# Attention's values as the stationary operand, two key heads in one bank, and mLSTM sums a step later

## The chip, the cores and the metric

The kernel runs on one core of a Trainium2 chip. The metric is the device time of one execution in microseconds (us). Five engines work side by side: TensorE (PE in the profile; its weight loads are PEld), VectorE (DVE), ScalarE (ACT), GpSimd (POOL) and SyncE (SP), which issues nearly all DMAs. Each engine takes its instructions in the order in which they stand, and waits where an operand isn't there.

## What is computed

A decoder trunk of two layers on 256 tokens of width 1024, in float32. The change lies in the mixer of each layer, between the two feed-forward blocks:

```python
u = rmsnorm(x); z = u @ W_in                       # q, k, v, gates of both mixers, merge gates
hA = mlstm(...)                                    # 4 heads, 128 values each
yA = (sigmoid(o) * rmsnorm(hA)) @ w_a
# sliding-window attention, 8 query heads, 2 key heads, 64 wide, window 128
m = max(max(logits), sink); pr = exp(logits - m)
denom = sum(pr) + exp(sink - m)
hB = einsum('bnkgqs,bnskd->bnqkgd', pr / denom, v)
yB = hB @ w_b
x = x + (sigmoid(gA) * yA + sigmoid(gB) * yB) @ W_out
```

## The kernel before

**Tiles.** The 256 tokens are two tiles of 128 (t = 0, 1). Every large product runs as three TensorE passes in a rounded float32 format (`mm_unit`): each weight matrix is loaded in units of up to 128x2048 (`raw`), ScalarE rounds it to `hi`, VectorE takes the rest as `lo`, and lo·xh + hi·xl + hi·xh is summed in PSUM. The stationary operand is the activation, turned so that features lie on the partitions; the moving one is 512 weight columns. `take` keeps three units ahead (`AHEAD = 3`); three raw buffers and four hi/lo buffers go round.

**Order.** TensorE's instructions stand in the order in which the code issues them. After each half unit (12 matmuls of one token tile) `stream` calls `tick`, which moves every spawned generator on by one `yield`. So side work (attention, mLSTM) is strewn between the halves of the projections, and the constants `W_...` say how many such steps a piece waits. The other engines' instructions are placed by the framework's scheduler, and then run in that order.

**The mixer.** `mix_in` projects `sq`, `if` (gates, keys, values), `mqk`, `mv`, `mo`, `ga0`, `ga1`, `gb0`, `gb1` (two units each, whose results are `z_mix_...`), then `w_b` (`yb`) and `w_a` (`ya`) for each half of the columns, then `w_out`. Beside the projections:

- Attention: `swa` normalises q and k, `swa_logits` multiplies them (`lg`, `L`), `swa_part` does the softmax. Token tile 0 is one part (8 heads, 128 keys), tile 1 two parts of four heads (256 keys, two key blocks kt). The probabilities `L` are turned to have keys on partitions: VectorE transposes 32x32 blocks into `inq_PT`, a DMA writes them to DRAM (`scr_PT`), a second reads them back in another order (`back_PT`), and a copy on ScalarE or VectorE puts them into `PT`. Of `back` there are two buffers, so that a second reading waits for the copy of the one before the last. Then `PT` is stationary and 64 columns of the values `vsw` move (`ov`, L721), one matmul for each head and key block. `hb` = `ov` times 1/denominator, and `hb` goes through the same turn (`inq_hb`, `scr_hb`, `back_hb`) before it is split into `abT`, the stationary operand of `yb`.
- mLSTM: `ml_mix` makes the weights `E` (E01, E2) from `st`; `ml_out` multiplies them by the values (`num`), divides, normalises (sums of squares `ssn`, with a GpSimd power `rn`), gates (`ha`), and turns `ha` through DRAM into the other half of `abT`, for `ya`.

`drain` finishes whatever is left of the generators ahead of `yb`.

Of the kernel before, what the change touches and what calls it, by code (L numbers as in the profile page):

```python
# [28 lines left out]
SWKV = 2  # L29
# [27 lines left out]
W_PT = 3  # L57
W_OV = 2
W_HB = 1
W_ST = 2  # L60
W_NUM = 1
W_HA = 3


@with_exitstack
def trunk_kernel(ctx: ExitStack, tc: tile.TileContext, a: dict, out: bass.AP):
# [50 lines left out]
    def by_cols(w, rows, cols, name):  # L117
# [48 lines left out]
    for i in range(DEPTH):  # L166
# [3 lines left out]
        for n in range(2):  # L170
            cols = [(512 * n, 512 * (n + 1))]
            specs.extend(by_cols(a["w_b"][i], 512, cols, f"wb{i}_{n}"))
            specs.extend(by_cols(a["w_a"][i], 512, cols, f"wa{i}_{n}"))
# [6 lines left out]
    def load_next(between=()):  # L180
# [8 lines left out]
        if between:  # L189
            src = srcs[0].rearrange("(k p) c -> p k c", p=P)  # L190
            for h, also in enumerate(between):
                ks = slice(h * kk // len(between), (h + 1) * kk // len(between))
                nc.sync.dma_start(rv[:, ks, :], src[:, ks, :])
                also()
        else:
            c0 = 0
            for s in srcs:
                w = s.shape[1]
                nc.sync.dma_start(rv[:, :, c0 : c0 + w], s.rearrange("(k p) c -> p k c", p=P))
                c0 += w  # L200
# [316 lines left out]
    def mix_in(pool, i, xn, finish):  # L517
# [127 lines left out]
        def swa_logits(t):  # L645
# [27 lines left out]
            for h0, L, mx in parts:  # L673
                gen = swa_part(t, h0, nh, L, mx)
                spawn(gen)
                advance(gen)

        def swa_part(t, h0, nh, L, mx):
            part = slice(h0, h0 + nh)
# [18 lines left out]
            rinv = stat("rinv")  # L698
            nc.vector.reciprocal(rinv, rs)
            for _ in range(W_PT):  # L700
                yield
# [11 lines left out]
            for _ in zip(*[turn_p(kt, j0) for kt in range(t + 1) for j0 in range(0, nh, 4)], strict=True):  # L713
                yield
            for _ in range(W_OV):
                yield
            ov = bank(f"ov{nmp}")[:, 0 : nh * HD]
            for j in range(nh):
                g = (h0 + j) // 4
                for kt in range(t + 1):  # L720
                    nc.tensor.matmul(  # L721
                        ov[:, j * HD : (j + 1) * HD],
                        PT[:, kt, j, :],
                        vsw[kt][:, g * HD : (g + 1) * HD],
                        start=kt == 0,
                        stop=kt == t,
                    )
            hb = work.tile([P, nh * HD], F32, tag="sg", name=f"hb{nmp}")
            nc.vector.tensor_tensor(
                heads(hb, HD), heads(ov, HD), rinv[:, :, None].broadcast_to([P, nh, HD]), op=ALU.mult  # L730
            )
            for _ in range(W_HB):
                yield
            ks = slice(h0 * HD // P, (h0 + nh) * HD // P)
            hi, lo = (part[:, ks, :] for part in abT[t][1])
            yield from back_split(blocks(hb), hi, lo, f"hb{nmp}")

# [87 lines left out]
        def ml_out(t, ha, E01, E2):  # L825
# [36 lines left out]
            nc.vector.tensor_tensor(haf, haf, go, op=ALU.mult)  # L862
# [189 lines left out]
```

## Time and profile before

| | |
|---|---|
| median of 3 runs | 1116.51 us (1115.41 to 1116.57) |
| profiled execution | 1116.3 us, of it 1114.4 us from first to last instruction |
| PE busy | 1101.9 us, 99% |
| DVE busy | 760.0 us, 68% |
| ACT busy | 585.7 us, 53% |
| DMA | 253.40 MB, 227 GB/s |
| mean granted TensorE clock | 0.998 |

The mixer of the first layer runs from about 200 to 350 us, that of the second from about 750 to 900. A row of the timeline gives the start in us from the span's start, the length of the group, engine, line, operation, tiles and shape; what stands in square brackets is idle time of that engine just before, with what ended it. Matmuls overlap in their records, so the time a matmul costs is the distance to the next one's start.

### The profile page before, as it was taken

The page shows a single profiled execution, that of the slowest core. Times are in us where ns is not written, and L with a number is a line of the kernel's source. Part 1 is how long each engine was busy: PE and PEld are TensorE (multiplying, and loading weights), DVE is VectorE, ACT ScalarE, POOL GpSimd, SP SyncE. Part 2 cuts the span into 40 slices and gives each one's busy share as a digit, 9 for nine tenths or more (in the row PEclk, how much of TensorE's full clock was granted, in tenths as well). Part 3 has the DMA queues.
Part 4 walks back from the last instruction along what each step waited for, and adds up shares of the span by engine and source line. Part 5 has one row for each costly group of instructions (what it writes and reads, how often), then busy time and mean ns, then how long its engine had stood idle before and what let it go on. Part 6 is the DMA issues. An engine that isn't in the chain of part 4 may idle for free.

```text
span 1114.4 us, 13451 instructions
## 1 busy us (share of the span) xinstructions
PE 1101.9 (99%) x5080; PEld 911.4 (82%) x5080; DVE 760.0 (68%) x962; ACT 585.7 (53%) x848; POOL 32.0 (3%) x30
## 2 busy tenths in 40 slices
PE   8999999999999999999999999999999999999998
PEld 7788888878878888888888888888787888888887
DVE  6775755689777666656776667556986777667564
ACT  6544544668545544444664454446784454445353
POOL 1000000100000000000000000001000000000000
PEclk9999999999999999999999999999999999999999
DMA  7888766777664867766757767666777557777661
GB/s 269 275 293 254 231 215 198 235 246 258 223 211 153 280 220 259 234 209 230 256 164 240 260 219 236 219 208 208 257 247 247 191 187 243 250 231 242 209 218 66
DMA packets 173026, 253.40 MB, mean 227 GB/s; under 512 B 18601, under 2 KB 72993, under 8 KB 172961
## 3 DMA queue, kind: packets, MB, share of 16 engines
q1 hardware_dynamic: 172960, 252.54, 68.9%
q8 instruction: 40, 0.66, 0.2%
q14 instruction: 26, 0.21, 0.1%
HBM read 228.64 MB, written 23.88 MB: 227 GB/s over the span
## 4 chain that ended last, share of the span: by engine, by line
PE 80%; DVE 10%; DMA 4%; issue 2%; ACT 2%; POOL 1%; SPq 0%; DVEq 0%
PE h_f L231 14%; PE h_f L233 14%; PE h_f L232 14%; PE acc_f_o L233 7%; PE acc_f_o L232 7%; PE acc_f_o L231 7%; DMA back_PT<-scr_PT 2%; PE acc_wout L233 1%; PE acc_wout L231 1%; PE acc_wout L232 1%; PE acc_pg L232 1%; PE acc_pg L233 1%; PE acc_pg L231 1%; DVE lo_z_ga L204 1%; DVE inq_PT L264 1%
## 5 line engine op out<-in xcount | busy, mean ns | idle before, releaser
L204 DVE TENSOR_TENSOR lo_f<-raw_f,hi_f 128x1024 fp32r<-128x1024 f32 (+1 forms) x176 | 207.6, 1215 | 83.6 <-ACT hi_f L203 83.1
L203 ACT CAST hi_f<-raw_f 128x1024 fp32r<-128x1024 f32 (+1 forms) x178 | 176.4, 1038 | 142.4 <-PE h_f L233 94.1
L204 DVE TENSOR_TENSOR lo_f_o<-raw_f_o,hi_f_o 128x1024 fp32r<-128x1024 f32 x88 | 104.2, 1219 | 71.1 <-ACT hi_f_o L203 71.1
L231 PE MATMUL h_f<-lo_f,xT_f_0h 128*128 128x512 f32 x352 | 138.0, 392 | 0.3 <-DVE lo_f L204 0.2
L232 PE MATMUL h_f<-hi_f,xT_f_0l 128*128 128x512 f32 x352 | 137.1, 390 | 1.1 <-DVE xT_f_0l L248 1.1
L231 PE MATMUL h_f<-lo_f,xT_f_1h 128*128 128x512 f32 x352 | 137.2, 390 | 0.5 <-DVE lo_f L204 0.4
L233 PE MATMUL h_f<-hi_f,xT_f_0h 128*128 128x512 f32 x352 | 137.0, 389 | 0.0
L232 PE MATMUL h_f<-hi_f,xT_f_1l 128*128 128x512 f32 x352 | 136.9, 389 | 0.0
L233 PE MATMUL h_f<-hi_f,xT_f_1h 128*128 128x512 f32 x352 | 136.9, 389 | 0.0
L203 ACT CAST hi_f_o<-raw_f_o 128x1024 fp32r<-128x1024 f32 x88 | 88.0, 1048 | 89.5 <-PE acc_f_o L233 52.9
L231 PEld LDWEIGHTS h_f<-lo_f,xT_f_0h 128*128 128x128 f32 x352 | 66.1, 188 | 15.0 <-issue 0.6
L231 PEld LDWEIGHTS h_f<-lo_f,xT_f_1h 128*128 128x128 f32 x352 | 66.1, 188 | 14.9 <-DVE lo_f L204 1.4
L232 PEld LDWEIGHTS h_f<-hi_f,xT_f_0l 128*128 128x128 f32 x352 | 66.1, 188 | 14.8 <-DVE xT_f_0l L248 1.4
L233 PEld LDWEIGHTS h_f<-hi_f,xT_f_1h 128*128 128x128 f32 x352 | 66.1, 188 | 13.8
L233 PEld LDWEIGHTS h_f<-hi_f,xT_f_0h 128*128 128x128 f32 x352 | 66.1, 188 | 13.7
L232 PEld LDWEIGHTS h_f<-hi_f,xT_f_1l 128*128 128x128 f32 x352 | 66.1, 188 | 13.7
L233 PE MATMUL acc_f_o<-hi_f_o,hT_f_1h 128*128 128x512 f32 x176 | 68.5, 389 | 0.0
L231 PE MATMUL acc_f_o<-lo_f_o,hT_f_0h 128*128 128x512 f32 x176 | 68.5, 389 | 0.0
L232 PE MATMUL acc_f_o<-hi_f_o,hT_f_0l 128*128 128x512 f32 x176 | 68.5, 389 | 0.0
L233 PE MATMUL acc_f_o<-hi_f_o,hT_f_0h 128*128 128x512 f32 x176 | 68.5, 389 | 0.0
L231 PE MATMUL acc_f_o<-lo_f_o,hT_f_1h 128*128 128x512 f32 x176 | 68.5, 389 | 0.0
L232 PE MATMUL acc_f_o<-hi_f_o,hT_f_1l 128*128 128x512 f32 x176 | 68.5, 389 | 0.0
(352 smaller groups left out, 2036.1 us busy)
## 6 DMA issues: line engine op xcount, KB each, us to landing
raw_f<-in_ffn_wi_dram SPq DMA_DIRECT2D x79, 1024.0 KB, 5.4
raw_f_o<-in_ffn_wo_dram SPq DMA_DIRECT2D x40, 1024.0 KB, 5.2
scr_h_f<-inq_h_f SPq DMA_DIRECT2D x40, 256.0 KB, 4.0
back_h_f<-scr_h_f SPq DMA_DIRECT2D x40, 256.0 KB, 5.0
raw_f<-in_ffn_wi_dram SPq DMA_DIRECT2D x18, 512.0 KB, 4.2
raw_z_ga<-in_w_in_dram SPq DMA_DIRECT2D x8, 1024.0 KB, 5.5
raw_z_gb<-in_w_in_dram SPq DMA_DIRECT2D x8, 1024.0 KB, 7.4
raw_wout<-in_w_out_dram SPq DMA_DIRECT2D x8, 1024.0 KB, 4.9
```

What stands on the lines that cost most here:

```text
L203: nc.scalar.copy(hi[:, o:e], raw[:, o:e])
L204: (nc.gpsimd if between and o // step % 2 == 0 else nc.vector).tensor_tensor(lo[:, o:e], raw[:, o:e], hi[:, o:e].bitcast(F32), op=ALU.subtract
L231: nc.tensor.matmul(o, xh, wl[:, k, sl], start=start, stop=False)
L232: nc.tensor.matmul(o, xl, wh[:, k, sl], start=False, stop=False)
L233: nc.tensor.matmul(o, xh, wh[:, k, sl], start=False, stop=stop)
L264: nc.vector.transpose(inq[:, 0:n].rearrange(f"p (b {order}) -> p b k s", b=4, k=k), src.rearrange("p k (c b) -> p b k c", b=4),)
```

## The change

Four things change in each layer's mixer.

1. The division by the softmax denominator moves ahead of the turn: `L` is multiplied by `rinv` on VectorE (128x1024 elements, three times a layer).
2. `ov` is turned round: 64 value columns of one key head are stationary, and the four heads' probabilities (512 columns of `PT`) move. Key head 0 writes PSUM partitions 0 to 63, key head 1 partitions 64 to 127 of one bank, so that the result has features on partitions already. `hb`, its turn and its DMAs go; `split_evac` splits `ov` into `abT` straight from PSUM. Both parts of tile 1 are now needed for its one `ov` group.
3. Since features are now grouped by key head, the rows of `w_b` are loaded in that order: two DMAs of 64 partitions (512 KB each) for a unit, in place of one of 128.
4. Steps: `W_OV` 2 to 4, `W_NUM` 1 to 2, and the waits `W_HB` (1) and `W_HA` (3) go.

```diff
-W_OV = 2
-W_HB = 1
+W_OV = 4
 W_ST = 2
-W_NUM = 1
-W_HA = 3
+W_NUM = 2
...
+    def by_heads(w, cols, name):
+
+        c0, c1 = cols
+        return [(f"{name}_0", 0, 4, [w[256 * g : 256 * (g + 1), c0:c1] for g in range(SWKV)], c1 - c0)]
...
-            specs.extend(by_cols(a["w_b"][i], 512, cols, f"wb{i}_{n}"))
+            specs.extend(by_heads(a["w_b"][i], cols[0], f"wb{i}_{n}"))
...
+                if s.shape[0] < kk * P:
+                    rows = slice(HD * g, HD * (g + 1))
+                    nc.sync.dma_start(rv[rows, :, :], s.rearrange("(k p) c -> p k c", p=HD))
+                    continue
...
             nc.vector.reciprocal(rinv, rs)
+            nc.vector.tensor_tensor(L, L, rinv[:, :, None].broadcast_to([P, nh, L.shape[2]]), op=ALU.mult)
...
+            turned += [PT[:, :, j0 : j0 + 4, :] for j0 in range(0, nh, 4)]
+            if len(turned) < SWKV:
+                return
             for _ in range(W_OV):
                 yield
-            ov = bank(f"ov{nmp}")[:, 0 : nh * HD]
-            for j in range(nh):
-                g = (h0 + j) // 4
-                for kt in range(t + 1):
+            ov = bank(f"ov{i}_{t}")
+            for kt in range(t + 1):
+                for g in range(SWKV):
+                    rows = slice(g * HD, (g + 1) * HD)
                     nc.tensor.matmul(
-                        ov[:, j * HD : (j + 1) * HD],
-                        PT[:, kt, j, :],
-                        vsw[kt][:, g * HD : (g + 1) * HD],
-                        start=kt == 0,
-                        stop=kt == t,
+                        heads(ov, P)[rows], vsw[kt][:, rows], turned[g][:, kt], start=kt == 0, stop=kt == t
                     )
-            hb = work.tile([P, nh * HD], F32, tag="sg", name=f"hb{nmp}")
-            nc.vector.tensor_tensor(
-                heads(hb, HD), heads(ov, HD), rinv[:, :, None].broadcast_to([P, nh, HD]), op=ALU.mult
-            )
...
-            yield from back_split(blocks(hb), hi, lo, f"hb{nmp}")
+            split_evac(*abT[t][1], blocks(ov))
...
-            for _ in range(W_HA):
-                yield
             yield from back_split(blocks(haf), *abT[t][0], f"ha{i}_{t}")
```

How this moves instructions is shown at three places of the first layer; the second layer is the same.

**TensorE, around `ov`.** Before, tile 0's eight `ov` matmuls stand ahead of the projection `gb0`'s first half unit, and tile 1's sixteen one half unit further on:

```order
L233 MATMUL z_mix_ga_1_2256<-hi_z_ga_4_2117,xT_mix_1_1h 128x512
L721 MATMUL ov_0_0_2399<-vsw_0_1555,PT_0_0_2136 128x64 x8
L231 MATMUL z_mix_gb_0_2412<-lo_z_gb_0_2191,xT_mix_0_0h 128x512
L232 MATMUL z_mix_gb_0_2412<-hi_z_gb_0_2190,xT_mix_0_0l 128x512
L233 MATMUL z_mix_gb_0_2412<-hi_z_gb_0_2190,xT_mix_0_0h 128x512
```

With the change tile 0's two matmuls stand two half units later, and tile 1's four another half unit on, between the two halves of `gb0`'s second unit:

```order
L240 MATMUL z_mix_gb_0_2412<-hi_z_gb_4_2261,xT_mix_0_1h 128x512
L735 MATMUL ov_1_2475<-PT_1_0_2178,vsw_0_1555 64x512
L735 MATMUL ov_1_2475<-PT_1_4_2185,vsw_0_1555 64x512
L735 MATMUL ov_1_2475<-PT_1_0_2178,vsw_1_1556 64x512
L735 MATMUL ov_1_2475<-PT_1_4_2185,vsw_1_1556 64x512
L238 MATMUL z_mix_gb_1_2413<-lo_z_gb_4_2262,xT_mix_1_1h 128x512
```

The `num` groups stand one half unit later than before (12 matmuls): tile 0's behind the first half of `ga1`'s second unit, tile 1's behind its second half.

**VectorE, where the probabilities are turned and copied back.** Before, the transposes of tile 1 (`inq_PT_1_...`) stand close together, ahead of the products of the mLSTM weights (`E` with `st`):

```order
L795 TENSOR_TENSOR E_0_2144<-Mb_1568,maskb 128x512
L699 RECIPROCAL rinv_1_0_2079<-rs_1_0_2073 128x4
L264 STREAM_TRANSPOSE inq_PT_1_0_0_0_2176<-L_1_0_2042 128x512
L697 TENSOR_TENSOR rs_1_4_2088<-rs_1_4_2088,es_1_4_2085 128x4
L699 RECIPROCAL rinv_1_4_2094<-rs_1_4_2088 128x4
L264 STREAM_TRANSPOSE inq_PT_1_0_1_0_2179<-L_1_0_2042 128x512
L204 TENSOR_TENSOR lo_z_ga_4_2118<-raw_z_ga_4_2116,hi_z_ga_4_2117 128x1024 x2
L264 STREAM_TRANSPOSE inq_PT_1_4_0_0_2183<-L_1_4_2044 128x512
L264 STREAM_TRANSPOSE inq_PT_1_4_1_0_2186<-L_1_4_2044 128x512
L811 TENSOR_TENSOR E_0_2143<-E_0_2143,st_0_2217 128x2x128
```

With the change the last two transposes come behind the multiplies by `rinv` (three of them are above this piece), behind these products and behind the `lo` of another unit:

```order
L271 STREAM_TRANSPOSE inq_PT_1_0_1_0_2182<-L_1_0_2043 128x512
L813 TENSOR_TENSOR E_0_2146<-E_0_2146,st_0_2220 128x2x128
L813 TENSOR_TENSOR E_0_2146<-E_0_2146,st_1_2221 128x2x128
L813 TENSOR_TENSOR E_0_2146<-E_0_2146,st_0_2220 128x2x128
L211 TENSOR_TENSOR lo_z_gb_0_2194<-raw_z_gb_0_2192,hi_z_gb_0_2193 128x1024 x2
L813 TENSOR_TENSOR E_0_2146<-E_0_2146,st_1_2221 128x2x128
L821 TENSOR_TENSOR E_0_2147<-E_0_2147,st_0_2230 128x128
L821 TENSOR_TENSOR E_0_2147<-E_0_2147,st_1_2231 128x128
L821 TENSOR_TENSOR E_0_2147<-E_0_2147,st_0_2230 128x128
L271 STREAM_TRANSPOSE inq_PT_1_4_0_0_2186<-L_1_4_2045 128x512
L821 TENSOR_TENSOR E_0_2147<-E_0_2147,st_1_2231 128x128
L271 STREAM_TRANSPOSE inq_PT_1_4_1_0_2189<-L_1_4_2045 128x512
```

The last copy into `PT` (`PT_1_4`), without which tile 1's `ov` can't end, stood behind `num`'s divisions before, and ahead of mLSTM's normalisation. With the change it stands behind the whole normalisation of mLSTM's tile 0 and a `lo`:

```order
L847 RECIPROCAL r_0_2323<-dd_0_2322 128x2 x2
L848 TENSOR_TENSOR ha_0_2240<-num_0_0_2326,r_0_2323 128x256
L848 TENSOR_TENSOR ha_0_2240<-num_0_1_2335,r_0_2323 128x256
L854 TENSOR_SCALAR vn_0_2344<-ssn_0_2324 128x4
L858 SCALAR_TENSOR_TENSOR ha_0_2240<-ha_0_2240,rn_0_2346,mlg_1551 128x128 x4
L864 TENSOR_TENSOR ha_0_2240<-ha_0_2240,gates_0_1559 128x512
L211 TENSOR_TENSOR lo_z_gb_4_2416<-raw_z_gb_4_2414,hi_z_gb_4_2415 128x1024
L720 COPY PT_1_4_2185<-back_PT_1_4_1_0_2190 128x512
```

**SP, ahead of `yb`.** Before, six DMAs of `hb` (`scr_hb`, `back_hb`) stand between the weight loads of `w_b`, `w_a` and `w_out`:

```order
L199 DMA raw_wa_0_0_2533<-in_w_a_dram 128x4x512
L270 DMA scr_hb_0_0_2474<-inq_hb_0_0_2434 128x512
L274 DMA back_hb_0_0_2435<-scr_hb_0_0_2474 128x4x128
L199 DMA raw_wb_1_0_2572<-in_w_b_dram 128x4x512
L270 DMA scr_ha_0_2482<-inq_ha_0_2459 128x512
L270 DMA scr_hb_1_0_2507<-inq_hb_1_0_2476 128x256
L199 DMA raw_wa_1_0_2614<-in_w_a_dram 128x4x512
L270 DMA scr_hb_1_4_2509<-inq_hb_1_4_2479 128x256
L270 DMA scr_ha_1_2511<-inq_ha_1_2484 128x512
L274 DMA back_ha_0_2460<-scr_ha_0_2482 128x4x128
```

With the change they are gone, and the two halves of a `w_b` unit stand apart, the second behind the readings of tile 1's probabilities:

```order
L281 DMA back_PT_1_0_1_0_2183<-scr_PT_1_0_1_0_2214 128x4x128
L204 DMA raw_wb_0_0_2454<-in_w_b_dram 64x4x512
L281 DMA back_PT_1_4_0_0_2187<-scr_PT_1_4_0_0_2216 128x4x128
L281 DMA back_PT_1_4_1_0_2190<-scr_PT_1_4_1_0_2218 128x4x128
L204 DMA raw_wb_0_0_2454<-in_w_b_dram 64x4x512
L206 DMA raw_wa_0_0_2503<-in_w_a_dram 128x4x512
L277 DMA scr_ha_0_2369<-inq_ha_0_2354 128x512
L204 DMA raw_wb_1_0_2537<-in_w_b_dram 64x4x512
L281 DMA back_ha_0_2355<-scr_ha_0_2369 128x4x128
L204 DMA raw_wb_1_0_2537<-in_w_b_dram 64x4x512
```

More of the change, by code (lines that the diff above doesn't have):

```diff
@@ L196, in load_next @@
             c0 = 0
-            for s in srcs:
+            for g, s in enumerate(srcs):
                 w = s.shape[1]
+                if s.shape[0] < kk * P:
+                    rows = slice(HD * g, HD * (g + 1))
+                    nc.sync.dma_start(rv[rows, :, :], s.rearrange("(k p) c -> p k c", p=HD))
+                    continue
                 nc.sync.dma_start(rv[:, :, c0 : c0 + w], s.rearrange("(k p) c -> p k c", p=P))
@@ L653, in swa_logits @@
             parts = []
+            turned = []
             for h0 in range(0, SWQ, nh):
@@ L673, in swa_logits, with swa_part @@
             for h0, L, mx in parts:
-                gen = swa_part(t, h0, nh, L, mx)
+                gen = swa_part(t, h0, nh, L, mx, turned)
                 spawn(gen)
                 advance(gen)
-        def swa_part(t, h0, nh, L, mx):
+        def swa_part(t, h0, nh, L, mx, turned):
             part = slice(h0, h0 + nh)
@@ L714, in swa_part @@
                 yield
+            turned += [PT[:, :, j0 : j0 + 4, :] for j0 in range(0, nh, 4)]
+            if len(turned) < SWKV:
+                return
             for _ in range(W_OV):
                 yield
-            ov = bank(f"ov{nmp}")[:, 0 : nh * HD]
-            for j in range(nh):
-                g = (h0 + j) // 4
-                for kt in range(t + 1):
+            ov = bank(f"ov{i}_{t}")
+            for kt in range(t + 1):
+                for g in range(SWKV):
+                    rows = slice(g * HD, (g + 1) * HD)
                     nc.tensor.matmul(
-                        ov[:, j * HD : (j + 1) * HD],
-                        PT[:, kt, j, :],
-                        vsw[kt][:, g * HD : (g + 1) * HD],
-                        start=kt == 0,
-                        stop=kt == t,
-                    )
-            hb = work.tile([P, nh * HD], F32, tag="sg", name=f"hb{nmp}")
-            nc.vector.tensor_tensor(
-                heads(hb, HD), heads(ov, HD), rinv[:, :, None].broadcast_to([P, nh, HD]), op=ALU.mult
-            )
-            for _ in range(W_HB):
-                yield
-            ks = slice(h0 * HD // P, (h0 + nh) * HD // P)
-            hi, lo = (part[:, ks, :] for part in abT[t][1])
-            yield from back_split(blocks(hb), hi, lo, f"hb{nmp}")
+                        heads(ov, P)[rows], vsw[kt][:, rows], turned[g][:, kt], start=kt == 0, stop=kt == t
+                    )
+            split_evac(*abT[t][1], blocks(ov))
         cem = small.tile([P, 16], F32, tag="cem", name=f"cem{i}")
@@ L862, in ml_out @@
             nc.vector.tensor_tensor(haf, haf, go, op=ALU.mult)
-            for _ in range(W_HA):
-                yield
             yield from back_split(blocks(haf), *abT[t][0], f"ha{i}_{t}")
```

## The prediction

> **What bounds the kernel now.** I read the page's busy times first, then what PE waited for, then the mixer's timeline.
>
> ```profile
> PE 1101.9 (99%) x5080; PEld 911.4 (82%) x5080; DVE 760.0 (68%) x962; ACT 585.7 (53%) x848; POOL 32.0 (3%) x30
> ```
>
> PE is busy from end to end; time goes only where PE's own work shrinks or a wait of PE goes. The list of PE's waits (engine, line, who is waited for: us in total, times, longest) is headed by two that this change can touch:
>
> ```profile
> PE yb L231 <- ACT abT_1h L247: 2.1, 3, 1.1
> PE yb L232 <- DVE abT_1l L248: 1.9, 2, 1.0
> ```
>
> The first stage behind the mixers, `yb`, waits for the attention output `abT_1`. What that costs in all is seen from starts in PE's timeline, the first layer and then the second:
>
> ```profile
> 302.35 0.39 PE L231 MATMUL yb<-lo_wb,abT_1h 128*128 128x512 f32 x1
> 302.57 0.39 PE L232 MATMUL yb<-hi_wb,abT_1l 128*128 128x512 f32 x1
> ...
> 306.99 0.50 PE L232 MATMUL yb<-hi_wb,abT_1l 128*128 128x512 f32 x1 [0.97 <-DVE abT_1l L248]
> ...
> 309.48 0.50 PE L231 MATMUL yb<-lo_wb,abT_1h 128*128 128x512 f32 x1 [1.06 <-ACT abT_1h L247]
> ...
> 311.21 0.39 PE L231 MATMUL ya<-lo_wa,abT_0h 128*128 128x512 f32 x1
> ...
> 313.93 0.39 PE L231 MATMUL ya<-lo_wa,abT_0h 128*128 128x512 f32 x1
> 314.61 0.50 PE L232 MATMUL ya<-hi_wa,abT_0l 128*128 128x512 f32 x1 [0.29 <-DVE abT_0l L248]
> ```
>
> ```profile
> 851.49 0.39 PE L231 MATMUL yb<-lo_wb,abT_1h 128*128 128x512 f32 x1
> ...
> 856.62 0.80 PE L232 MATMUL yb<-hi_wb,abT_1l 128*128 128x512 f32 x1 [0.97 <-DVE abT_1l L248]
> ...
> 860.79 0.39 PE L231 MATMUL ya<-lo_wa,abT_0h 128*128 128x512 f32 x1
> ```
>
> A matmul of 512 columns costs 0.227 us (302.35 to 302.57). The 24 of `yb` should take 5.4 us. They take 8.9 in the first layer (302.35 to 311.21), 3.4 too many, and 9.3 in the second (851.49 to 860.79), 3.9 too many. Idle time proper is less than that. In the second layer the view by stages shows the rest (length, PE busy, its rows, granted clock, DMA):
>
> ```profile
> 851.90:856.60 4.70, 2.98 (x12) 1.00 0.51 184
> 856.60:860.10 3.50, 3.48 (x8) 0.52 0.70 249
> ```
>
> For 3.5 us after the waits the granted clock is 0.52, and only eight matmuls are done. At half speed 3.5 us do the work of 1.8, so a wait of PE can cost itself and 1.7 us more. The Trainium skill, "TensorE: Matmul & The Clock Gate" (section "What's actually happening"), puts this to a window of about 3.4 us with too little activity, which runs freely; the length agrees, and the first layer, with more idle time and no slow stretch, agrees with the chance in it.
>
> **The change, part by part.** *`ov` on PE.*
>
> ```profile
> 275.16 1.89 PE L721 MATMUL ov<-vsw,PT 128*128 128x64 f32 x16
> 276.86 0.48 PE L231 MATMUL z_mix_gb<-lo_z_gb,xT_mix_0h 128*128 128x512 f32 x1
> 277.18 0.39 PE L232 MATMUL z_mix_gb<-hi_z_gb,xT_mix_0l 128*128 128x512 f32 x1
> ...
> 279.70 3.68 PE L721 MATMUL ov<-vsw,PT 128*128 128x64 f32 x32
> 283.19 0.48 PE L231 MATMUL z_mix_gb<-lo_z_gb,xT_mix_0h 128*128 128x512 f32 x1
> ```
>
> Before: 1.70 + 3.49, and 0.09 behind each (276.86 to 277.18 in place of 0.227): 5.4 us a layer. Each plain-f32 matmul shows as two passes (8 matmuls, 16 rows). The trace has no column groups. Nearest are mLSTM's `st` products, which use 64 rows each, side by side:
>
> ```profile
> 256.85 0.39 PE L233 MATMUL z_mix_ga<-hi_z_ga,xT_mix_1h 128*128 128x512 f32 x1
> 257.17 0.49 PE L807 MATMUL st<-qkT 64*128 64x256 f32 x2
> ...
> 257.17 1.13 PE L807 MATMUL st<-qkT 64*128 64x256 f32 x8
> 258.14 0.61 PE L815 MATMUL st<-qkT 64*128 64x128 f32 x8
> 258.68 0.50 PE L231 MATMUL z_mix_ga<-lo_z_ga,xT_mix_1h 128*128 128x512 f32 x1
> 259.02 0.39 PE L232 MATMUL z_mix_ga<-hi_z_ga,xT_mix_1l 128*128 128x512 f32 x1
> ```
>
> Two start within 0.01 us, so they run together; eight of 256 columns, four pairs, take 0.97, of which about 0.1 is the start: 0.21 a pair and pass, so 0.43 for 512 columns. Going in and out costs 0.09 (256.85 to 257.17), 0.1 at the start, 0.1 at the end and 0.11 (258.68 to 259.02): 0.4 a visit. With pairs: tile 0 two passes, 0.85 + 0.4; tile 1 four, 1.7 + 0.4. That is 3.4 a layer, a gain of 2.0; **4.0 for both**. Bounds: nothing for the visit, 5.7; no pairing, -1.3 (below). I take the pairs, since row groups are the nearest thing and run so.
>
> *`hb` and its way through DRAM go.* Off PE, `abT` now needs only a ScalarE and a VectorE pass over `ov`, which ends near 287 us, 14 us ahead of `yb`. The `hb` DMAs no longer hold the `back` buffers and ScalarE's queue ahead of `hi_wb`. So the `yb` excess goes, 3.4 + 3.9, and with `ha` turned three steps sooner (W_HA) less the one of W_NUM, `ya`'s 0.68 for 0.23 and as much as 0.1 behind it: **7.9**. Next late would be `lo_wb`: the second half of its unit now waits on SP behind the last `back_PT` (about 281 us), and lands some 5 us later; with 2.4 us of VectorE it is there by 293, 8 us early. The extra DMA issues cost SP 0.4 each, under that cover. Bounds: 6 (one wait of some 2 us comes back) to 7.9.
>
> *Multiplies and later transposes.* The VectorE sum hardly changes: three multiplies are added; `hb`'s product, transposes and smaller splits go. The order matters. VectorE's timeline:
>
> ```profile
> 262.17 2.09 DVE L264 STREAM_TRANSPOSE inq_PT<-L 128x512 f32<-128x512 f32 x2
> 264.17 1.38 DVE L811 TENSOR_TENSOR E<-E,st 128x256 f32<-128x256 f32 x4
> ...
> 265.86 2.36 DVE L204 TENSOR_TENSOR lo_z_gb<-raw_z_gb,hi_z_gb 128x1024 fp32r<-128x1024 f32 x2
> ...
> 268.52 0.43 DVE L711 COPY PT<-back_PT 128x512 f32<-128x512 f32 x1
> ...
> 275.95 0.75 DVE L846 TENSOR_TENSOR ha<-num,r 128x256 f32<-128x256 f32 x2
> ...
> 281.00 0.43 DVE L711 COPY PT<-back_PT 128x512 f32<-128x512 f32 x1 [2.20 <-DMA back_PT<-scr_PT]
> ...
> 282.62 1.14 DVE L856 SCALAR_TENSOR_TENSOR ha<-ha,rn,mlg 128x128 f32<-128x128 f32 x4 [1.12 <-POOL rn L302]
> 283.80 0.69 DVE L862 TENSOR_TENSOR ha<-ha,gates 128x512 f32<-128x512 f32 x1
> ```
>
> Two of ScalarE's squares for the normalisation, one head each, and the way of a `back_PT` reading from issue to landing:
>
> ```profile
> 280.48 0.31 ACT L850 ACTIVATE jn<-ha 128x128 f32<-128x128 f32 x1
> ...
> 280.92 0.31 ACT L850 ACTIVATE jn<-ha 128x128 f32<-128x128 f32 x1
> ```
>
> ```profile
> DMA to landing us min/median/max: 2.6/5.0/5.8
> ```
>
> The last two transposes started at 262.17. Now three multiplies stand ahead of them (no such row; nearest is a `lo` of the same size, two in 2.36, so 3.4 for three, some tenths in doubt), the `E` products (264.17 to 265.86, 1.7) and a `lo` pair (2.3): they start at 269.6 and end near 272. Another `lo` pair follows, to 274.3, then the copy of tile 0's probabilities, done at 274.8 (it started at 268.52 before). It frees the `back` buffer that the second reading of tile 1's first part needs; that lands 2.6 to 5.8 us later, 277.4 to 280.6, and is copied in 0.43. Then, new in VectorE's order, comes the normalisation of mLSTM's tile 0: divisions 1.0, four squares on ScalarE 0.44 apart, 1.8, a small operation 0.2, GpSimd's power 1.1, `ha` 1.1, the gate 0.7, one `lo` 1.1, 7.0 in all. Then the last copy, done between 285.3 and 288.5.
>
> When does PE need it? Before, half a unit beside `ov` takes 2.8 (276.86 to 279.70); two halves behind 283.19 end at 288.75. Less 5.2 of the old `ov`, plus 1.25 of tile 0's new one, is 284.8, and tile 1's fourth matmul, which needs the copy, issues 0.2 + 0.85 later, near 285.9. So PE waits **0 to 2.6 us**, in both layers alike; less than nothing is excluded, since no wait of PE stands at `ov` now. The reading at 274.8 has only the tail of a 1 MB load ahead of it, which speaks for the lower half of its way: I take 1.0 a layer, **2.0 for both**. Behind the waiting matmul stand the rest of `gb0` and `gb1`, so the wait is paid in full.
>
> *`num`, a step later.* It started 1.4 us behind the end of the `E` products (264.17 + 1.38):
>
> ```profile
> 266.97 1.05 PE L838 MATMUL num<-vaug,E 128*128 128x129 f32 x8
> ```
>
> It now comes half a unit, 2.7, later; the products come 3.6 later (3.4 of multiplies and a `lo` pair of 2.3 ahead of the last, less two transposes of 2.1 now behind). That leaves 0.5: no wait, and 0.5 of one at the worst. The step itself only moves work that PE does anyway.
>
> **Sum**: 4.0 + 7.9 - 2.0 = 9.9 off the profiled execution's 1116.3 (1.9 of it outside the span), 0.2 below the median: **1106.4 us**. Own range 1103.0 (no wait at `ov`, visits nearly free) to 1109.6 (2.6 us of wait in each layer).
>
> **Rivals.** *Column groups don't pair.* Then each visit has twice the passes: 1.7 + 0.4 and 3.4 + 0.4, 5.9 for 5.4 before: a loss of 0.5 a layer, 5.0 worse than forecast: **1111.4**. For it: no such pair is in the trace. Against: `st`.
>
> *Bare loads.* If besides no weight load of a column group ran under a matmul, 12 loads a layer would come on top, each like this row's 188 ns:
>
> ```profile
> L231 PEld LDWEIGHTS h_f<-lo_f,xT_f_0h 128*128 128x128 f32 x352 | 66.1, 188 | 15.0 <-issue 0.6
> ```
>
> That is 4.5 more: **1115.9**. Against: 82% of PEld beside 99% of PE, which shows loads running under matmuls of the same rows all the time. The Trainium skill, "TensorE: Matmul & The Clock Gate" (Part 3, "The mechanism"), has the rule that gives this rival: a load overlaps matmuls in flight only where its row group differs, and column groups share theirs. The same part reports 2.38 times the speed for three column tiles, against both rivals; no run so far shows either.
>
> *The last copy is late by the whole bound*, 2.6, and the idle time brings the slow clock, 1.7: 4.3 a layer for 1.0, 6.6 worse: **1113.0**. For it: the second layer's slow stretch followed on waits of this size. Against: the median way of a reading, 5.0, includes readings behind large loads.
>
> *Slower.* The same mechanism further on: mLSTM's squares wait in ScalarE's order behind copies of `back_PT`, so that both readings and the 7 us run strictly behind one another. What is gained before it is 11.9, 5.9 a layer; with the slow clock it decides from a wait of 4.2 us. At 6 us (the copy at 292) each layer pays 7.7: **1119.8**. For it: all three are in one in-order queue; against: the readings would have to exceed their maximum of 5.8.
>
> *It doesn't free `yb`*: `lo_wb` or `ha` lands late and about 2 us a layer stay: **1110.4**.
>
> **How the numbers follow.** Forecast 0.63, no pairs 0.12, bare loads 0.03, late copy 0.12, slower 0.05, `yb` not freed 0.05. Range 1103.0 to 1112.5: from no wait at all and free visits (1104.4 less 1.6) past the unpaired case; it leaves out bare loads, the late copy and the slower case, 0.2. A measurement here tells about 0.2%, 2.2 us, from no change: below 1114.1 is faster. Forecast, no pairs, not freed and 0.08 of the late copy are faster, 0.88; the rest of the late copy and bare loads are within, 0.07; slower 0.05.
>
> **What would show it.** Right: `ov` rows in twos starting together, about 0.9 us for tile 0 and 1.7 for tile 1; no `yb` wait on `abT_1`; no stretch with a granted clock near 0.5 at 855; a wait of `ov` on DVE `PT` of about 1 us. Wrong: rows 0.43 apart one by one; `ov` waits above 2 us or a slow clock behind them; `yb` waiting for `lo_wb`.

## The result, and the profile after

The changed kernel takes **1109.38 us**, median of 4 runs (1108.48 to 1111.12); beside it on the same chip the kernel before takes 1116.54 (1115.41 to 1118.61, 4 runs). The ratio is **0.994, 95% interval 0.9924 to 0.9955**: 7.2 us faster, where 10.1 less than the median of before was forecast. It lies in the forecast's range, 3.0 us above the forecast itself. The profiled run is one of the four, the longest: 1111.12, with a span of 1109.3.

The page's first line of numbers, engines with busy time, share and instructions:

```profile
PE 1097.1 (99%) x5008; PEld 902.4 (81%) x5008; DVE 759.5 (68%) x954; ACT 585.6 (53%) x846; POOL 31.7 (3%) x30
```

PE still bounds the kernel and does 4.8 us less. The list of PE's waits (who is waited for: us in total, times, longest), from its top:

```profile
PE h_f L239 <- DVE xT_f_0l L255: 2.2, 1, 2.2
PE ov L735 <- DVE PT L720: 1.6, 2, 1.1
```

`yb` is gone from it, and `ov` has come in, waiting for the last copy of the probabilities, as forecast. The other row is in the first stage of the program. PE's timeline from the end of the mixer, first layer:

```profile
304.96 0.39 PE L238 MATMUL yb<-lo_wb,abT_1h 128*128 128x512 f32 x1
...
310.40 0.39 PE L238 MATMUL ya<-lo_wa,abT_0h 128*128 128x512 f32 x1
```

`yb` takes 5.44 us, 24 times 0.227, and no more. PE's timeline around `ov`, tile 0, then tile 1 in both layers:

```profile
283.49 0.39 PE L240 MATMUL z_mix_gb<-hi_z_gb,xT_mix_0h 128*128 128x512 f32 x1
283.81 1.08 PE L735 MATMUL ov<-PT,vsw 128*64 128x512 f32 x4
284.82 0.50 PE L238 MATMUL z_mix_gb<-lo_z_gb,xT_mix_1h 128*128 128x512 f32 x1
285.16 0.39 PE L239 MATMUL z_mix_gb<-hi_z_gb,xT_mix_1l 128*128 128x512 f32 x1
...
287.77 1.93 PE L735 MATMUL ov<-PT,vsw 128*64 128x512 f32 x6
290.20 1.07 PE L735 MATMUL ov<-PT,vsw 128*64 128x512 f32 x2 [0.50 <-DVE PT L720]
291.20 0.50 PE L238 MATMUL z_mix_gb<-lo_z_gb,xT_mix_1h 128*128 128x512 f32 x1
```

```profile
832.37 1.93 PE L735 MATMUL ov<-PT,vsw 128*64 128x512 f32 x6
835.36 1.07 PE L735 MATMUL ov<-PT,vsw 128*64 128x512 f32 x2 [1.06 <-DVE PT L720]
836.36 0.50 PE L238 MATMUL z_mix_gb<-lo_z_gb,xT_mix_1h 128*128 128x512 f32 x1
```

Tile 0's four passes are over in 1.01 us: two pairs. Tile 1's eight fall into six and two, with a wait between them.

Since the run as a whole moves by some us from one execution to the next, the stages are the better measure. They run here from the first matmul of one name to the first of another in PE's timeline (`gp` is the gates' transposes, ahead of everything that the change moves); "again" is a second profile of the changed kernel, from the experiments:

| stage, us | before | after | after, again |
|---|---|---|---|
| start to `gp`, layer 0 | 216.50 | 219.63 | 216.64 |
| `gp` to `yb`, layer 0 | 85.85 | 85.33 | 86.05 |
| `yb` to `ya` | 8.86 | 5.44 | 5.44 |
| `ya` to `tp_mx` | 11.49 | 10.88 | 10.88 |
| to `gp` of layer 1 | 442.96 | 442.92 | 442.89 |
| `gp` to `yb`, layer 1 | 85.83 | 85.89 | 86.16 |
| `yb` to `ya` | 9.30 | 5.44 | 5.44 |
| `ya` to `tp_mx` | 11.18 | 10.88 | 10.88 |
| to the end | 242.44 | 242.91 | 242.91 |
| span | 1114.4 | 1109.3 | 1107.3 |

The gain is all in `yb` and `ya`: 7.3 and 0.9. From `gp` to `yb`, where `ov` is cheaper and waits, the sum is nothing: -0.5 in the first profile, +0.5 in the second. And the first profile's start is 3.1 us later than before's.

### The profile page after: what moved, and what is told of

The parts are those of the page before. It is cut to its first block, busy times and chain, and to the rows that moved or that the text cites. A ratio compares the mean times of both kernels' runs of the same rounds, so it can differ in the third digit from the quotient of the medians.

```text
span 1109.3 us, 13267 instructions
## 1 busy us (share of the span) xinstructions
PE 1097.1 (99%) x5008; PEld 902.4 (81%) x5008; DVE 759.5 (68%) x954; ACT 585.6 (53%) x846; POOL 31.7 (3%) x30
## 4 chain that ended last, share of the span: by engine, by line
PE 87%; DVE 6%; ACT 3%; issue 2%; DMA 1%; POOL 1%; SPq 0%; DVEq 0%; ACTq 0%
PE h_f L238 14%; PE h_f L239 14%; PE h_f L240 14%; PE acc_f_o L238 7%; PE acc_f_o L240 7%; PE acc_f_o L239 7%; PE acc_wout L238 1%; PE acc_wout L240 1%; PE acc_wout L239 1%; PE acc_pg L240 1%; PE acc_pg L239 1%; PE acc_pg L238 1%; PE z_mix_gb L238 1%; PE z_mix_gb L240 1%; PE z_mix_gb L239 1%
```

## The experiments

Twelve kernels, four at a time on one chip, each four beside runs of the kernel before (1115.98, 1116.42 and 1116.18 us, medians of 11, 9 and 11 runs). Diffs are against the changed kernel. Where a run's time and its stages say different things, the stages are given.

**`ov` one more step later.**

```diff
-W_OV = 4
+W_OV = 5
```

> The changed kernel with ov one more step (half a unit, 2.7 us) later, W_OV 5 in place of 4. In the changed kernel's trace tile 1's ov visit is 1.6 us longer in the first layer and 2.1 us in the second than four pair passes take, because its last passes wait for VectorE's last copy of PT. Theory (that wait is paid in full, and nothing else is late): both go, 3.7 us less than the changed kernel's 1109.4: about 1105.7. Rival (the wait only moves: abT_1 of tile 1 comes some 2 us later and yb waits for it, or the last copy moves along): 1108.5 to 1110, with yb waiting for abT_1.

Measured: 1108.8 us (1107.08 to 1109.86, 5 runs), ratio 0.9937 (0.9924 to 0.9949). No wait at `ov`; `gp` to `yb` 83.82 and 83.77, which is 1.5 and 2.1 less than in the changed kernel, 3.6 in all, as the theory says. But `ya` to `tp_mx` grows by 0.3 in each layer, and the stages behind it, to the next `gp` and to the end, by 0.9 each. In the list of PE's waits two rows are new:

```profile
PE tp_mx L261 <- DVE ma L894: 0.9, 2, 0.7
PE tp_mx L261 <- ACT hi_wout L210: 0.7, 1, 0.7
```

So both were half right: the wait is paid in full, and 2.5 of the 3.6 come back, not at `yb` but one stage further on. `abT_1` of tile 1 now stands between the two halves of `wa`'s split on ScalarE and VectorE. Which row of it makes `ma` late was not tried.

**The new form with the old steps.**

```diff
-W_OV = 4
+W_OV = 2
-W_NUM = 2
+W_NUM = 1
+W_HA = 3
...
+            for _ in range(W_HA):
+                yield
             yield from back_split(blocks(haf), *abT[t][0], f"ha{i}_{t}")
```

> The changed kernel with the old steps: W_OV 2, W_NUM 1, W_HA 3, so the new form of ov alone. Theory (the form makes the probabilities late, and the moved steps are what hides it): tile 1's ov stands 5.4 us earlier in PE's order and the last copy of PT hardly moves, so ov waits 4 to 7 us a layer in place of 1.6 and 2.1, and num waits for the E products, 1 to 4 us; 1115 to 1125, about 1119, slower than before the change. Rival (the steps matter little, since the round trip of hb that is gone is the whole gain): within 2 us of the changed kernel's 1109.4.

Measured: 1120.05 us (1118.88 to 1121.81, 5 runs), ratio 1.0038 (1.0025 to 1.0052): slower than before the change. PE's waits, and the view by stages (length, engines' busy time, granted clock, DMA share) behind the first layer's wait:

```profile
PE ov L736 <- ACT PT L719: 5.8, 2, 2.9
PE num L841 <- DVE E L814: 2.7, 2, 1.4
```

```profile
287.20:291.00 3.80, 3.56 (x7) 0.58 (x7) 3.67 (x11) 3.80 (x8) 1.01 (x1) 0.57 0.25 52
```

`ov` sits idle 2.9 a layer and then runs at a granted clock of 0.57 (0.51 in the second layer, from 837.2 to 840.7 us), and its tile 1 visits are 5.7 and 5.5 longer than one without a wait (1.87, shown further on); `gp` to `yb` is 91.17 and 90.81, while `yb` and `ya` are as short as in the changed kernel. The form alone loses more than it gains; the later steps turn it round. It is a case like the prediction's slower rival, though by another way: a long wait at `ov` with the slow clock behind it eats the whole gain.

**Heads outside, key tiles inside** (with `ov` a step later, so that no wait covers anything).

```diff
-            for kt in range(t + 1):
-                for g in range(SWKV):
-                    rows = slice(g * HD, (g + 1) * HD)
+            for g in range(SWKV):
+                rows = slice(g * HD, (g + 1) * HD)
+                for kt in range(t + 1):
```

> As e1, with ov's loops exchanged: all of key head 0's matmuls ahead of key head 1's, so that in tile 1 the two column groups are neighbours in the order only once. Theory (each column group runs its own matmuls as they come, as the second layer of the changed kernel suggests, where head 1's first pass started 0.36 us behind head 0's and ahead of head 0's second): tile 1 still takes about 2.1 us and the time is that of e1, about 1105.7. Rival (only neighbours in the order run together): two passes more of 0.43 us a layer, 1.7 us for both: e1 and 1.7, about 1107.4, with rows 0.43 apart one by one.

Measured: 1109.01 us (1106.72 to 1109.81, 5 runs), ratio 0.9935 (0.9923 to 0.9948); `gp` to `yb` 83.84 and 83.77, within 0.02 of the run with `ov` a step later. The theory holds in the stages: the column groups need not be neighbours in the order. The time lies above what either side named, for what comes back behind `ya` in this run too, and for a late start (219.00).

**One stationary of 128 columns, no column groups** (also with `ov` a step later).

```diff
-            ov = bank(f"ov{i}_{t}")
+            ovs = [bank(f"ov{i}_{t}_{g}") for g in range(SWKV)]
             for kt in range(t + 1):
                 for g in range(SWKV):
...
+                    nc.tensor.matmul(heads(ovs[g], P), vsw[kt], turned[g][:, kt], start=kt == 0, stop=kt == t)
+            for g in range(SWKV):
+                rows = slice(g * HD, (g + 1) * HD)
+                hi, lo = abT[t][1]
+                split_evac(hi[rows], lo[rows], blocks(ovs[g])[rows])
```

> As e1, with the values of both key heads as one stationary of 128 columns and a bank of its own for each head, of which half the rows are used: no column groups, so no pairs and no change of tile size, twice the passes. Theory (the pairs are worth what the trace shows): 12 passes of 0.43 us and 0.2 of starts, 5.3 us a layer in place of 3.3: e1 and 4.1, about 1109.8. Rival (the pairs save little because the visits to column groups cost as much): within 1 us of e1.

Measured: 1112.27 us (1110.98 to 1114.02, 7 runs), ratio 0.997 (0.9959 to 0.998). `gp` to `yb` is 85.70 and 85.61, 1.9 and 1.8 more than with pairs. PE's timeline of tile 1, without groups here and with them in the run with heads outside:

```profile
290.46 3.59 PE L734 MATMUL ov<-PT,vsw 128*128 128x512 f32 x8
```

```profile
289.91 1.94 PE L735 MATMUL ov<-PT,vsw 128*64 128x512 f32 x8
```

Eight passes of 512 columns take 3.59 one after the other and 1.94 in pairs. The pairs are worth 3.7 us for both layers, net of what a visit to the column groups costs; 4.1 was expected.

**`num` at its old step.**

```diff
-W_NUM = 2
+W_NUM = 1
```

> The changed kernel with num one step earlier again, W_NUM 1. Of the prediction this tests that num's step is free. Theory (the step is needed, since the E products end late behind the multiplies): in the changed kernel's trace E's products for tile 0 end at 272.2, and num, at 272.8, would stand half a unit earlier, near 270.1; PE waits some 2 us a layer there. In return mLSTM's normalisation runs ahead, VectorE's last copy of PT is early and ov's waits of 1.6 and 2.1 go. Sum about 0: 1109 to 1110.5, with num waiting for DVE E and no wait at ov. Rival (num's wait comes on top, ov's wait stays): 1113 to 1114. Second rival (num hides even without the step): 1105.7.

Measured: 1107.97 us (1107.69 to 1110.3, 5 runs), ratio 0.9926 (0.9914 to 0.9939). The first row of PE's waits:

```profile
PE num L840 <- DVE E L813: 2.7, 2, 1.3
```

`ov` does not wait at all, and `gp` to `yb` is 85.43 and 85.37: +0.1 and -0.5 against the first profile of the changed kernel, -0.6 and -0.8 against the second. The theory's sum of about nothing holds in the stages of the first; the time is 1 us below what it named. The step of `num` is a trade: without it `num`'s first group takes 1.6 longer in each layer (2.4 us to the next unit for 0.8; the list counts the idle 1.3 alone), and with it mLSTM's normalisation stands where VectorE's last copy of `PT` has to come behind it.

**The last copy on ScalarE.**

```diff
-                if kt + j0 == 0:
+                if kt + j0 == 0 or h0:
                     nc.scalar.copy(dst, b)
```

> The changed kernel with the last copy of PT (tile 1, key head 1, second block) on ScalarE in place of VectorE, where it no longer stands behind mLSTM's normalisation but behind one hi cast. Theory (ov waits for the copy's place in VectorE's queue, not for the data, which landed at 287.4 where ov needed them at 288.7): the copy ends near 289.1, so the first layer's ov wait falls from 1.6 to about 0.4 and the second's from 2.1 to about 0.5; about 2.8 less than the changed kernel, 1106.6. Rival (the wait is for the reading itself, or what ScalarE loses comes back at tp_mx, as the stages behind ya grew by 2.5 us in the run with ov a step later): 1108.5 to 1109.4.

Measured: **1106.96 us** (1106.87 to 1108.38, 4 runs), ratio 0.9916 (0.9903 to 0.993). `gp` to `yb` is 84.83 and 85.04, 0.5 and 0.85 less than in the first profile of the changed kernel, 1.2 and 1.1 less than in the second; nothing comes back later. ScalarE's timeline:

```profile
283.75 1.04 ACT L210 CAST hi_z_gb<-raw_z_gb 128x1024 fp32r<-128x1024 f32 x1
284.68 0.62 ACT L718 COPY PT<-back_PT 128x512 f32<-128x512 f32 x1
...
285.32 1.05 ACT L210 CAST hi_z_gb<-raw_z_gb 128x1024 fp32r<-128x1024 f32 x1
286.25 0.63 ACT L718 COPY PT<-back_PT 128x512 f32<-128x512 f32 x1
```

The direction is the theory's, the size about half of it: the last copy now stands behind a cast, and ends at 286.9, still 1.0 us after `ov` wanted it.

**No multiplies.** The three products with `rinv` are left out.

```diff
             nc.vector.reciprocal(rinv, rs)
-            nc.vector.tensor_tensor(L, L, rinv[:, :, None].broadcast_to([P, nh, L.shape[2]]), op=ALU.mult)
```

> The changed kernel without the three multiplies by rinv: the probabilities stay without their division by the row sums. Theory (the multiplies ahead of the transposes are what makes the last copy of PT late): the transposes of PT start 2 to 3 us earlier, the ov waits of 1.6 and 2.1 fall below 0.5 each, and the time is 1105.5 to 1106.5. Rival (VectorE has idle time before the last copy anyway, and the copy is bound to mLSTM's normalisation, whose start num's step sets): ov still waits 1 us or more a layer, and the time is 1108.5 to 1109.4.

Measured: 1105.8 us (1104.16 to 1106.88, 4 runs), ratio 0.9904 (0.9887 to 0.9921). No wait at `ov`, `gp` to `yb` 83.80 and 83.75. Tile 1's visit is the one without a wait, by which the others are read:

```profile
285.50 0.39 PE L240 MATMUL z_mix_gb<-hi_z_gb,xT_mix_1h 128*128 128x512 f32 x1
285.82 1.94 PE L734 MATMUL ov<-PT,vsw 128*64 128x512 f32 x8
287.69 0.50 PE L238 MATMUL z_mix_gb<-lo_z_gb,xT_mix_1h 128*128 128x512 f32 x1
288.03 0.40 PE L239 MATMUL z_mix_gb<-hi_z_gb,xT_mix_1l 128*128 128x512 f32 x1
```

From the first pass to the next unit it is 1.87 us. In the changed kernel the same stretch is 3.43 and 3.99 (287.77 to 291.20, 832.37 to 836.36): waits of 1.56 and 2.12. So without the multiplies there is no wait, as the theory says. The edit frees more than their own 3.6 us, though: VectorE's order is then that of the kernel before, with the last two transposes ahead of the `E` products, and the first of them starts at 263.34, 8.2 us earlier than in the changed kernel (273.50, less 2.0 of that profile's later start) and not 2 to 3. It is the multiplies together with the order that comes with them.

**`ha` turned three steps later again.**

```diff
+W_HA = 3
...
+            for _ in range(W_HA):
+                yield
             yield from back_split(blocks(haf), *abT[t][0], f"ha{i}_{t}")
```

> The changed kernel with the three steps ahead of the turning of ha put back (W_HA 3). Of the prediction this tests that ya's gain (0.6 in the first layer and 0.3 in the second between ya's first matmul and the stage behind it) comes from ha being turned sooner, and that yb needs nothing of ha. Theory: yb stays at 5.4 us in both layers; ya waits for abT_0, since its reading would land 8 us later than in the changed kernel, where it left 5.1 us ahead of its use for tile 1: 2 to 6 us more a layer, 1113 to 1121. Rival (only hb's round trip held the back buffers, and ha has slack enough): within 1 us of 1109.4.

Measured: 1109.34 us (1109.04 to 1110.23, 4 runs), ratio 0.9936 (0.9923 to 0.995). `ya` to `tp_mx` is 10.88 in both layers, as in the changed kernel. The theory falls, by much: the steps do nothing for `ya`. The run with the old steps has 10.88 too, so the gain comes with the new form. That it is `hb`'s way through DRAM, and nothing else of the form, was not tested apart.

**The changed kernel again**, unchanged.

> The changed kernel as it is, once more. Its first profile reached the stage gp 219.6 us after the start, as three of the experiments did (219.0 to 219.1), and four others, which differ from it only behind that point, 216.6 to 217.7. Theory (a change of some 2.6 us in the first stage that comes and goes with when the first load lands, and no effect of the change): from gp to the end the stages take the same times as in the first profile, 889.7 us, and the median lies between 1108.2, the first profile's 1111.1 less 2.9, and 1111.1. Rival (the late start belongs to the changed code): gp at 219 again in this profile, and a median near 1111.

Measured: 1110.75 us (1109.01 to 1112.1, 6 runs), ratio 0.9945 (0.9924 to 0.9965). `gp` comes at 216.64, so the late start does not belong to the code (of the eight experiments before, five and not four had come early). From `gp` to the end it is 890.7 where 889.7 was expected: `ov` waits longer in this profile.

```profile
284.83 1.93 PE L735 MATMUL ov<-PT,vsw 128*64 128x512 f32 x6
287.96 1.07 PE L735 MATMUL ov<-PT,vsw 128*64 128x512 f32 x2 [1.20 <-DVE PT L720]
288.96 0.50 PE L238 MATMUL z_mix_gb<-lo_z_gb,xT_mix_1h 128*128 128x512 f32 x1
```

284.83 to 288.96 is 4.13, a wait of 2.26; in the second layer it is 2.43, read in the same way.

**The multiplies just ahead of their own transposes.**

```diff
-            nc.vector.tensor_tensor(L, L, rinv[:, :, None].broadcast_to([P, nh, L.shape[2]]), op=ALU.mult)
             for _ in range(W_PT):
                 yield
+            nc.vector.tensor_tensor(L, L, rinv[:, :, None].broadcast_to([P, nh, L.shape[2]]), op=ALU.mult)
```

> The changed kernel with each multiply by rinv behind the W_PT steps, just ahead of its own transposes, so that VectorE turns tile 1's first part before it multiplies the second. Theory (the last copy of PT comes late through the multiplies ahead of the first part's transposes, as the run without multiplies bears out): the transposes of that part start 1.2 us earlier, the reading and the normalisation with them, and ov waits about 0.5 us a layer in place of 1.6 and 2.1; 1106 to 1107, as against 1108.2 to 1109.4 of the changed kernel. Rival (the second part's transposes, which the last multiply now delays, set the last copy): ov waits as before or more; 1109 to 1111.

Measured: 1107.82 us (1107.19 to 1110.16, 6 runs), ratio 0.9924 (0.9902 to 0.9946). `gp` to `yb` is 84.71 in the first layer and 86.18 in the second: in the first the wait of `ov` falls to 0.9; in the second it is 1.6, and `num`'s second group is 0.9 longer. There VectorE stands idle 2.9 us ahead of the last pair of transposes, until a write out of `inq_PT` is done. Right for one layer, wrong for the other.

**Both: late multiplies and the last copy on ScalarE.** The two diffs together.

> The run with late multiplies and the last copy of PT on ScalarE, where it stands right behind the other copy of that part. Theory (the two remedies add up): no wait at ov, gp to yb 83.8 us as in the run without multiplies, 1105.5 to 1106.5, the fastest of all with the right result. Rival (ScalarE's copy now waits for its reading ahead of a hi cast and holds ScalarE up): 1107 or more, with z_mix_gb waiting for hi_z_gb.

Measured: 1107.67 us (1105.13 to 1108.82, 6 runs), ratio 0.9916 (0.9896 to 0.9937). `gp` to `yb` is 83.80 in the first layer, no wait at all, and 85.21 in the second, where `ov` waits for ScalarE's first copy of that part: the theory for one layer, and a time in the rival's range, but `z_mix_gb` does not wait for `hi_z_gb`. This and the run with the copy alone have the two lowest medians of those that do the whole work: this one is 3.1 below the changed kernel beside it, the other 9.5 below the kernel before beside it. Their intervals still overlap with the changed kernel's, so it is the stages that carry this, not the medians.

**Late multiplies and `num` at its old step.**

> The run with late multiplies and num one step earlier (W_NUM 1). Theory (num's wait of 1.3 to 1.4 us a layer in the run with that step comes from a multiply ahead of the E products): E's products end 1.2 us earlier only if the last multiply stood ahead of them; here it still does, between the transposes and E, so num's wait stays near 1.3 and ov has none: gp to yb 85.4, 1107.5 to 1108.5. Rival (the multiplies' place does move E): num waits less than 0.5, gp to yb 84.3, about 1106.

Measured: 1109.59 us (1109.13 to 1110.69, 6 runs), ratio 0.9937 (0.9918 to 0.9957). `num` sits idle 2.7 in all, `ov` not at all, `gp` to `yb` 85.40 and 85.43, as the theory has it; its time is 1 us above what was named, with a late start (219.13) in its profile.

## Why the prediction was right, and where its size was off

In us against the kernel before, by the prediction's terms, with the two profiles of the changed kernel:

| term | forecast | first | again |
|---|---|---|---|
| `ov` on PE | -4.0 | -4.2 | -4.2 |
| new wait of `ov` | +2.0 | +3.7 | +4.7 |
| waits of `yb` and `ya` | -7.9 | -8.2 | -8.2 |
| `num` | 0 | 0 | 0 |
| sum | -9.9 | -8.7 | -7.7 |

The sums are those of the mixers' stages in the table above (-8.65 and -7.66).

*`ov` on PE.* Right, mechanism and size. Tile 0, from 283.49 to 285.16 less two spacings of 0.227, costs 1.2; tile 1 without a wait, from 285.50 to 288.03, costs 2.1. That is 3.3 a layer for a forecast of 3.4, out of 5.4. Taking the row groups of `st` as the nearest thing to column groups was right. What no pairs would have cost is seen in the run with 128 columns, 1.9 a layer more. (The prediction's bound for no pairs, -1.3, should have been -1.0 by its own rival.) The bare loads fell too. The Trainium skill, "TensorE: Matmul & The Clock Gate" (Part 3, "The mechanism"), has the rule that a load overlaps matmuls in flight only when the row group differs. By that rule alone the loads of the column groups would stand beside the matmuls; the trace disagrees, since PE's weight loads stand under running passes here.

```profile
288.25 0.14 PEld L735 LDWEIGHTS ov<-PT,vsw 128*64 128x64 f32 x1 [0.29 <-issue]
288.68 0.14 PEld L735 LDWEIGHTS ov<-PT,vsw 128*64 128x64 f32 x1 [0.29 <-issue]
```

They are 0.43 apart, as the passes themselves are, and that is what a pass costs alone (in the run without groups the first of eight starts at 290.46 and the last at 293.46), so these loads cost nothing.

*`yb` and `ya`.* The size is right, and `yb`'s reason: the stages are 3.4, 3.9, 0.6 and 0.3 shorter, and the stretch at half clock in the second layer is gone. Of `ya`'s reasons one was wrong. "`ha` turned three steps sooner (W_HA)" does nothing, as the run with the steps back shows; the new form is enough, so the size of `ya` is right in part by luck. The cover was also thinner than claimed. VectorE's timeline of the first layer:

```profile
298.69 1.22 DVE L211 TENSOR_TENSOR lo_wb<-raw_wb,hi_wb 128x1024 fp32r<-128x1024 f32 x1
...
301.58 0.65 DVE L255 TENSOR_TENSOR abT_1l<-ov,abT_1h 128x512 fp32r<-128x512 f32 x1
```

`abT_1` is complete at 302.2, 2.7 ahead of `yb` and not 14, since the passes over `ov` stand behind other work in both queues; `lo_wb` comes 5 ahead and not 8 (the forecast's own terms, 281, 5 and 2.4, add up to 288.4 and not 293). Nothing was lost by it here. That the thin cover is why a further step of `ov` gave most of its gain back is likely, not shown.

*The new wait of `ov`.* **This is the step that was mis-sized**: the mechanism is the one forecast, 1.0 a layer was taken out of 0 to 2.6, and 1.6 to 2.4 came. VectorE's timeline in the first profile:

```profile
278.00 0.40 DVE L720 COPY PT<-back_PT 128x512 f32<-128x512 f32 x1
...
282.39 0.23 DVE L846 TENSOR_TENSOR dd<-dd,cem 128x2 f32<-128x2 f32 x2 [1.72 <-ACT dd L845]
282.71 0.43 DVE L720 COPY PT<-back_PT 128x512 f32<-128x512 f32 x1
283.05 0.23 DVE L847 RECIPROCAL r<-dd 128x2 f32<-128x2 f32 x2
...
285.52 0.17 DVE L854 TENSOR_SCALAR vn<-ssn 128x4 f32<-128x4 f32 x1 [1.44 <-ACT jn L852]
...
288.59 1.22 DVE L211 TENSOR_TENSOR lo_z_gb<-raw_z_gb,hi_z_gb 128x1024 fp32r<-128x1024 f32 x1
289.73 0.42 DVE L720 COPY PT<-back_PT 128x512 f32<-128x512 f32 x1
```

Less the 3.1 of the late start, the copy of tile 0 ends at 275.3, where 274.8 was forecast, and from the end of the copy at 282.71 to the last one it is 6.6, where 7.0 was forecast. What the forecast chose was the reading between them. A wait of 1.0 stands for a reading of 4.2 us (274.8, 4.2, 0.43, 7.0 and 0.43 make 286.9), the middle of 2.6 to 5.8, because "only the tail of a 1 MB load" lay ahead of it. In the first profile its issue is the second of two in SP's timeline:

```profile
274.66 1.50 SPq L277 DMA_DIRECT2D scr_PT<-inq_PT  x2
276.28 2.52 SPq L281 DMA_DIRECT2D back_PT<-scr_PT  x2
278.85 0.66 SPq L204 DMA_DIRECT2D raw_wb<-in_w_b_dram  x1
```

It lasts 0.37 like the others and ends at 278.80, so it began at 278.43, and the copy followed 4.3 later at 282.71. There the last copy ends at 290.15, 287.0 without the late start, just where a wait of 1.0 had it (286.9); but PE was there some 0.3 earlier than forecast, and takes up to 0.1 to go on, and the visit shows 1.6. In the other three visits the reading is longer, and the waits are 2.1 to 2.4. In the first layer of the second profile it takes 5.1 us, issue to copy:

```profile
280.08 0.23 DVE L846 TENSOR_TENSOR dd<-dd,cem 128x2 f32<-128x2 f32 x2 [2.43 <-ACT dd L845]
280.48 0.43 DVE L720 COPY PT<-back_PT 128x512 f32<-128x512 f32 x1 [0.16 <-DMA back_PT<-scr_PT]
```

```profile
275.41 0.37 SPq L281 DMA_DIRECT2D back_PT<-scr_PT  x1
275.83 0.66 SPq L204 DMA_DIRECT2D raw_wb<-in_w_b_dram  x1
```

A half of `w_b` is issued 0.4 behind the reading, but that alone does not stretch it. In the second layer of the run with late multiplies it stands there too (the second reading of the first row starts at 821.64), and the reading takes 2.8:

```profile
818.70 3.31 SPq L281 DMA_DIRECT2D back_PT<-scr_PT  x2
822.06 0.61 SPq L204 DMA_DIRECT2D raw_wb<-in_w_b_dram  x1
```

```profile
824.44 0.43 DVE L720 COPY PT<-back_PT 128x512 f32<-128x512 f32 x1 [0.56 <-DMA back_PT<-scr_PT]
```

What differs is the 1 MB load of `z_gb` ahead. There it had landed 1.4 us before the reading was issued; in the two visits above it landed 1.1 and 1.4 us after. So the tail that was taken to be short is what goes with the long readings. No run varied it by itself.

There is also a path that the forecast did not have. Ahead of the copy VectorE sits idle 1.7 and 2.4 us (the rows of `dd`) for a small operation on ScalarE, and that stands behind ScalarE's own copy, out of the other reading:

```profile
281.67 0.62 ACT L718 COPY PT<-back_PT 128x512 f32<-128x512 f32 x1 [5.08 <-DMA back_PT<-scr_PT]
```

That other reading is issued on SP behind the writes of the last two transposes, which are late through VectorE's order, and takes 5.3 to 6.2 us in the four visits. This path ends only 0.1 to 0.2 us ahead of the one that was forecast. Had the forecast's reading alone been shorter, the wait would have been shorter by no more than that.

The bound of 2.6 held in all four visits, and no slow clock came behind the waits, as the view by stages shows for the first layer:

```profile
287.00:292.00 5.00, 4.50 (x15) 1.71 (x14) 4.97 (x11) 2.54 (x5) 0.00 (x0) 1.00 0.86 254
```

One reading of the views would have hidden half of it. PE's list of waits has 1.6 for `ov`, but the visits are 3.7 longer. While the second head's last passes wait, the first head's run alone (six passes in a row, then two), and PE counts as busy.

*Multiplies and `num`.* Without the multiplies there is no wait, and with them there is none either where `num`'s step is taken back, or in one layer where they stand late and the last copy is on ScalarE. So it takes both: the multiplies, with the order that they bring, and mLSTM's normalisation ahead of the last copy. `num`'s step costs nothing itself, as forecast, but what it does is trade one wait for another.

*What is left.* From 1116.3 by the measured sums one comes to 1107.6 and 1108.6, and another 0.5 lies at the very end: from the landing of the last output to the end of the span it is 1.5, where it was 1.1 before, with no work of the kernel left; why is not known. The medians are 1109.4 and 1110.8. The rest may lie in the first stage of the program, whose end came at 216.5 in the profile that the forecast started from, and at 219.0 to 219.6 in five of the thirteen profiles of the changed kernel and its variants. The changed kernel's own ten runs point the same way: the five with a mean granted clock of 0.999 or more took 1108.5 to 1109.5, the five with 0.998 or less 1110.1 to 1112.1. How often each kernel starts late isn't known: of before there is one profile. That part stays open.

## What to carry to other kernels

A product moved ahead of a transpose is cheap by the busy time and dear by the order: 1.2 us three times on an engine that is 68% busy became 3.7 to 4.7 us of waits on the one that is full, because a copy then stood behind an unrelated chain. Where a range for a wait hangs on one DMA, work out how much of the load ahead is left when it is issued: over the 24 visits with multiplies, 1.1 to 1.8 us left went with readings of 4.3 to 5.3 us from issue to copy, 0.6 to 0.8 with 4.0 to 4.8, and less with 2.8 and 3.2. Follow the other in-order queues to the same instruction too; here a second one came within 0.2 us. And after removing a wait, measure the stages behind it: one more step for `ov` gained 3.6 us and lost 2.5 a stage later.

## What the hardware showed that was not expected

Column groups take their own matmuls in their own order. With all of head 0's matmuls ahead of head 1's in the program, the eight passes of tile 1 still ran as four pairs (1.94 us).

The first stage decides 3 us from one execution to the next, and the PE clock has the larger share. The changed kernel's first profile and its second, by stages (the granted clock is the last number but two):

```profile
12.00:16.00 4.00, 3.89 (x10) 3.07 (x11) 1.71 (x7) 1.01 (x4) 1.08 (x2) 0.57 1.04 353
```

```profile
11.00:15.00 4.00, 3.80 (x21) 2.83 (x20) 2.95 (x8) 1.40 (x5) 1.40 (x3) 1.00 1.05 390
```

In the first PE had waited 2.2 us just ahead of it, in the second 1.3 (`h_f` for `xT_f_0l`, in the lists of waits). Ten matmuls are done in the one stretch and twenty-one in the other. All five late starts have a wait of 2.2 there and a granted clock near 0.5 behind it; the eight profiles with a wait of 1.1 to 1.3 have neither. It is not the wait's length alone: the run without multiplies also waited 2.2 there, kept a granted clock of 1.00 from 10 to 18 us, and reached `gp` at 217.66. So of the 3.0 between the two profiles about 1.0 goes with the longer wait and 2.0 with the clock. Why the clock fell in five of the six is open.
